# Hybrid decoder layer on one core: half-array products emitted in turn, the overfull test behind the output, and a last norm without GpSimd

## The chip, the core and the metric

The kernel runs on one core of a Trainium2 chip. The metric is the time of one execution in microseconds (us); smaller is better. Everything is float32. The engines are PE (matmuls), DVE (vector), ACT (scalar), POOL (GpSimd) and SP, which here only issues transfers.

## The reference, cut to what matters

One layer over 512 tokens of width 1024: three token mixers in parallel behind one input projection, an output projection and a layer norm, then 32 experts of which each token takes four, and a second layer norm.

```python
p = h @ w_in[l]                                   # 1024 -> all mixers' columns
y_pool = pool_mixer(p_pool, ...)
y_rwkv, v_first = rwkv7_mixer(p_rwkv, ...)        # 6 heads of 64
y_mlstm = mlstm_mixer(p_mlstm, ...)               # 6 heads of 64
mix = jnp.concatenate([y_pool, y_rwkv, y_mlstm], axis=-1) @ w_out[l]
h = layer_norm(DEEPNORM_ALPHA * h + mix, ln1_g[l], ln1_b[l])
ffn = moe_ffn(h, router_w[l], router_b[l], w_gate_up[l], b_gate_up[l], w_down[l], b_down[l])
h = layer_norm(DEEPNORM_ALPHA * h + ffn, ln2_g[l], ln2_b[l])
...
bonus = jnp.sum(rh * kh * rk, -1, keepdims=True) * vh      # in rwkv7_mixer
```

## The kernel before

**Mixer, about 0 to 400 us.** The 512 tokens are four tiles of 128 (`NT`). `x` and the weights are split into a high and a low part, so each product of the input projection is three matmuls (L222 to L224, or L249 to L251 for the mLSTM's values in `ml_vo`). `ml_vo` takes its columns in the rounds 2, 0, 1 of 256; a round holds four PSUM banks, tagged "pi" and "pm", until ACT evacuates them (L256). `self.bank()` alone takes a bank of the tag "ps".

The RWKV part goes over three head pairs `j`. `rwkv_prep(j)` makes the scaled keys and values, the bonus product (L596, evacuated by L597) and then the flips, transposes on PE (L604 and after). `rwkv_scores(j)` makes for each token tile four 128x128 products for each of two heads. A head has 64 features, so each product uses 64 of the array's 128 rows: `hh` 0 the upper half, `hh` 1 the lower (L652). DVE masks the products out of PSUM (L655 to L657), and PE uses the masked tile in L662 and L663. For the last pair, products L637 of both halves come first, in turn. `rwkv_base` is a serial chain of 31 steps on DVE (L693, L695); its result takes a round trip by DMA, is transposed (L699), and `rwkv_inv` begins with L756. `ml_scores` has half-array products of the same kind (L373).

**Experts, about 400 to 1455 us.** 402 MB of weights stream through a ring of SBUF chunks on SP's queue (L1171). Before the ring is free, its chunks are tiles of the mixer, so a load waits until the mixer lets go of its slot. POOL gathers tokens and adds the results to `yd` in DRAM.

**Tail.** `tail_rows` adds `yd` to the four residual tiles `res` by accumulating DMAs (L1507), with the loads of the norm's vectors between them (L1510), all on POOL's queue. `overflow` is an If on the count of the fullest expert (L1408 loads it on each engine, L1409 branches); it is not taken on these inputs. Then `tail`: PE scatters the last expert's results into eight banks (L1524, L1527), DVE adds them to `res` (L1531), ACT sums squares (L1537), and `scales` and `apply` end the norm. Tiles 0 and 1 use ACT (L1559), DVE (L1560) and GpSimd (L1561); tiles 2 and 3 use DVE (L1546, L1557). SP stores each half tile (L1562).

A scheduler decides the order in which each engine gets its instructions; each engine then runs them in that order.

Of the kernel before, what the change touches and what calls it, by code (L numbers as in the profile page):

```python
# [29 lines left out]
AF = mybir.ActivationFunctionType  # L30
# [96 lines left out]
class Trunk:  # L127
# [100 lines left out]
    def ml_vo(self):  # L228
# [9 lines left out]
        for q in (2, 0, 1):  # L238
# [4 lines left out]
            ps = [self.bank("pi" if i < 2 else "pm") for i in range(NT)]  # L243
# [114 lines left out]
    def ml_scores(self, i):  # L358
# [8 lines left out]
        for h in range(6):  # L367
            self.exp_ins = nc.scalar.activation(DW[:, h], DW[:, h], AF.Exp, bias=self.Q[:, i, 0, h:h + 1])
        for g in range(2):
            p = self.bank("pi")  # L370
            r = slice(64 * g, 64 * g + 64)
            for j in range(3):
                nc.tensor.matmul(p[:, j * 128:j * 128 + 128], self.k2[j][r, t], self.q2[j][r, t], start=True, stop=True)  # L373
            d = DW[:, g:6:2]
            nc.vector.scalar_tensor_tensor(d, p[:, :384].rearrange("p (j t) -> p j t", j=3), 1.0 / 32, d, OP.mult, OP.mult)
# [170 lines left out]
    def rwkv_prep(self, j):  # L546
# [12 lines left out]
        nc.tensor.matmul(p, self.w2t[0:64, j * 128:(j + 1) * 128], self.wdad[0:64], start=True, stop=True)  # L559
# [11 lines left out]
        pa = self.bank()  # L571
        nc.tensor.matmul(pa, self.w2t[64:128, j * 128:(j + 1) * 128], self.wdad[64:128], start=True, stop=True)
# [46 lines left out]
        for hh in range(2):  # L619
            rr = slice(64 * hh, 64 * hh + 64)  # L620
            for i in range(NT - 1):
                nc.vector.tensor_copy(self.H[i][rr, j], p[rr, 128 * i:128 * i + 128][:, rr])
        self.pj[j] = (at, bt, kt, cj)

    def rwkv_scores(self, j, first=False):
# [16 lines left out]
        for i in range(NT):  # L642
            ti = slice(i * 128, i * 128 + 128)
            tm = self.sp.tile([128, 2, 2, 128], F32, name="mkv", tag="mkv", bufs=2)
            (mab, mrb), yrk = self.M[i], self.Yrk[i]
            for hh in range(2):
                hd = 2 * j + hh
                rows = slice(64 * hh, 64 * hh + 64)
                p = self.bank()
                for q in range(1 if first else 0, 4):  # L650
                    lh, rh = prods[q]
                    nc.tensor.matmul(p[:, 128 * q:128 * q + 128], lh[rows, ti], rh[rows, ti], start=True, stop=True)  # L652
                pq = p.rearrange("p (q t) -> p q t", q=4)
# [536 lines left out]

    def expert_gather(self, e):
        x = self.xg[e % 2]
        self.nc.gpsimd.indirect_dma_start(out=x[0:CAP], out_offset=None, in_=self.hd,  # L1193
                                          in_offset=bass.IndirectOffsetOnAxis(ap=self.gidx[:, e:e + 1], axis=0),
                                          bounds_check=T - 1, oob_is_err=False)
        return x
# [151 lines left out]
    def experts(self):  # L1348
        self.xg = [self.mw.tile([128, D], F32, name=f"xg{q}") for q in range(2)]
        for x in self.xg:  # L1350
            self.nc.gpsimd.memset(x[0:CAP], 0.0)
# [3 lines left out]
        for e in range(NE):  # L1355
# [36 lines left out]
    def overflow(self):  # L1392
# [15 lines left out]
        most = nc.values_load(self.mxi[0:1, 0:1], min_val=0, max_val=T)  # L1408
        with tc.If(most > CAP):  # L1409
# [102 lines left out]
    def tail(self, out):  # L1512
# [167 lines left out]
```

## Time and profile before

| | |
|---|---|
| median of 3 runs | 1492.03 us (1488.74 to 1493.71) |
| the profiled execution | 1492.41 us |
| its span in the trace | 1490.7 us |
| PE busy | 1345.4 us, 90% |
| DVE, ACT, POOL busy | 466.6, 290.7, 228.2 us |
| data moved | 461.67 MB, 310 GB/s on average |

The span runs from the first to the last event of the trace; the profiled time is 1.7 us longer. Busy shares are averages over the three stages, which have different limits, so they are read stage by stage. Of matmuls the records overlap: two in flight at once count once as busy time, and a record lasts longer than the step from one to the next.

### The profile page before, as it was taken

What the parts mean: (1) busy time and instruction counts of PE and PEld (TensorE: products, weight loads), DVE (VectorE), ACT (ScalarE), POOL (GpSimd) and SP (SyncE); (2) the same over time, 40 slices, a digit from 0 to 9 for tenths busy, and PEclk for the clock granted to TensorE, in tenths of its full rate; (3) what the DMA queues carried; (4) which work ended last, traced back from release to release, by engine and by line L of the source; (5) the groups of instructions that cost most, each with busy time, mean ns of one, the idle gap of its engine ahead of it and who ended that gap; (6) DMA issues with size and microseconds to landing.
All of it is one profiled execution on the core that took longest, in us unless ns stands there. A gap on an engine that the chain in (4) does not pass through costs nothing. (4 is left out here: it accounts for less than half of the span.)

```text
span 1490.7 us, 19988 instructions
## 1 busy us (share of the span) xinstructions
PE 1345.4 (90%) x7852; PEld 639.2 (43%) x7853; DVE 466.6 (31%) x1108; ACT 290.7 (20%) x611; POOL 228.2 (15%) x206
## 2 busy tenths in 40 slices
PE   7899989998899999988799999999879888899993
PEld 5677888876533433232233333333323222333322
DVE  4867497697831212111111111111111110211115
ACT  4444243353211111111001111111100110111103
POOL 1111137142301010001001111011100100010111
PEclk9999888799899999999999999999999999999996
DMA  7222123355689999999999999999999999999964
GB/s 250 70 57 71 36 68 89 118 159 205 256 341 396 393 383 404 402 398 390 395 399 398 394 398 399 402 395 391 392 387 398 395 401 394 404 396 412 401 223 127
DMA packets 95232, 461.67 MB, mean 310 GB/s; under 512 B 18137, under 2 KB 26745, under 8 KB 45962
## 3 DMA queue, kind: packets, MB, share of 16 engines
q1 hardware_dynamic: 79674, 434.57, 74.1%
q0 software_dynamic: 10880, 21.32, 6.6%
q10 hardware_dynamic: 4560, 4.15, 0.9%
q8 instruction: 82, 1.34, 0.4%
q14 instruction: 36, 0.29, 0.1%
HBM read 445.97 MB, written 18.10 MB: 311 GB/s over the span
## 5 line engine op out<-in xcount | busy, mean ns | idle before, releaser
L1268 PE MATMUL gu<-wc,xT 128*64 128x512 f32 x2048 | 486.6, 606 | 67.0 <-DMA wc<-w_gate_up 64.4
L1268 PEld LDWEIGHTS gu<-wc,xT 128*64 128x64 f32 x2048 | 143.0, 138 | 392.9 <-issue 239.5
L1281 DVE TENSOR_SCALAR glu<-gu 128x256 f32<-128x256 f32 (+1 forms) x64 | 35.6, 556 | 843.8 <-PE gu L1273 391.5
L1314 PE MATMUL dn<-wc,aT 128*64 128x512 f32 x1024 | 247.6, 603 | 4.2 <-PEq L1261 2.4
L1282 ACT ACTIVATE glu<-glu 128x256 f32<-128x256 f32 (+1 forms) x64 | 33.6, 525 | 549.6 <-DVE glu L1281 549.4
L1193 POOL DMA_INDIRECT xg<-hd,gidx x31 | 31.3, 1009 | 665.0 <-PE tr L1207 659.7
L1314 PEld LDWEIGHTS dn<-wc,aT 128*64 128x64 f32 x1024 | 65.8, 136 | 117.6 <-issue 101.3
L1319 POOL DMA_INDIRECT yd<-eo,sidx x45 | 70.1, 1557 | 276.1 <-ACT eo L1318 276.1
L1273 PE MATMUL gu<-wc,xT 128*32 128x512 f32 x960 | 111.3, 596 | 0.0
L222 PE MATMUL pi<-xhi,whi 128*128 128x512 f32 x152 | 63.7, 419 | 8.9 <-ACT whi L172 8.9
L1208 ACT ACTIVATE xT<-tr 128x384 f32<-128x384 f32 x62 | 29.9, 490 | 177.2 <-PE tr L1207 177.2
L223 PE MATMUL pi<-xlo,whi 128*128 128x512 f32 x152 | 62.8, 413 | 0.6 <-DVE xlo L173 0.6
L1273 PEld LDWEIGHTS gu<-wc,xT 128*32 128x32 f32 x960 | 27.7, 109 | 79.3 <-issue 79.3
L224 PE MATMUL pi<-xhi,wlo 128*128 128x512 f32 x152 | 61.7, 406 | 0.0
L173 POOL TENSOR_TENSOR wlo<-wraw,whi 128x512 fp32r<-128x512 f32 (+1 forms) x28 | 39.3, 1407 | 134.9 <-ACT whi L172 129.4
L1318 ACT ACTIVATE eo<-dn,gate 128x512 f32<-128x512 f32 (+1 forms) x45 | 28.0, 621 | 162.9 <-PE dn L1314 84.4
L1309 PE MATMUL dn<-wc,aT 128*32 128x256 f32 x960 | 56.1, 381 | 1.0 <-ACT aT L1296 1.0
L172 ACT ACTIVATE whi<-wraw 128x512 fp32r<-128x512 f32 (+1 forms) x54 | 33.9, 631 | 56.4 <-DMA wraw<-w_in 25.3
L1309 PEld LDWEIGHTS dn<-wc,aT 128*32 128x32 f32 x960 | 29.5, 110 | 33.3 <-issue 13.8
L1284 DVE SCALAR_TENSOR_TENSOR glu<-glu 128x256 f32<-128x256 f32 (+1 forms) x64 | 35.6, 556 | 8.4 <-ACT glu L1282 7.1
L1295 PEld LDWEIGHTS tr<-ident,glu 128*128 128x128 f32 x192 | 25.7, 208 | 28.0 <-DVE sel L1214 19.5
L222 PEld LDWEIGHTS pi<-xhi,whi 128*128 128x128 f32 x152 | 29.5, 194 | 18.2 <-ACT whi L172 8.6
(489 smaller groups left out, 1585.8 us busy)
## 6 DMA issues: line engine op xcount, KB each, us to landing
wc<-w_gate_up SPq DMA_DIRECT2D x256, 1024.0 KB
wc<-w_down SPq DMA_DIRECT2D x128, 1024.0 KB
wraw<-w_in SPq DMA_DIRECT2D x46, 256.0 KB
wraw<-w_out SPq DMA_DIRECT2D x16, 256.0 KB
xraw<-xT SPq DMA_DIRECT2D x4, 512.0 KB
res<-x SPq DMA_DIRECT2D x4, 512.0 KB
hd<-res ACTq DMA_DIRECT2D x4, 512.0 KB
res<-yd POOLq DMA_DIRECT2D x4, 512.0 KB
```

Of the source, the lines that this page charges most:

```text
L172: self.hi_ins = nc.scalar.activation(hi, src, AF.Copy)
L173: return (eng or nc.vector).tensor_tensor(lo, src, hi, OP.subtract)
L222: nc.tensor.matmul(p, hi, xh, start=(k == 0), stop=False)
L223: nc.tensor.matmul(p, hi, xl, start=False, stop=False)
L224: nc.tensor.matmul(p, lo, xh, start=False, stop=(k == NK - 1))
L1268: mm(p[q][64 * h:64 * h + 64], xT[:, k, 0:64], w[:, 1024 * q + 512 * h:1024 * q + 512 * h + 512], start=False, stop=(k == NK - 1))
L1273: self.nc.tensor.matmul(p[2][32 * c:32 * c + 32], xT[:, k, 64:96], w4[:, c], start=False, stop=(k == NK - 1), skip_group_check=True)
L1281: nc.vector.tensor_scalar(out[:, c], g, 7.0, None, OP.min)
L1284: nc.vector.scalar_tensor_tensor(out[:, c], ln[:, c], 1.0, out[:, c], OP.add, OP.mult)
L1309: mm(p2[32 * c:32 * c + 32], aT[:, 4 + k % 2, 32 * (k // 2):32 * (k // 2) + 32], wd[k][:, 256 * c:256 * c + 256], start=(k == 0), stop=(k ...
L1314: mm(p0[64 * h:64 * h + 64], aT[:, k % 4, 64 * (k // 4):64 * (k // 4) + 64], wd[k][:, 512 * h:512 * h + 512], start=(k == 0), stop=(k == N ...
L1319: return nc.gpsimd.indirect_dma_start(out=self.yd.rearrange("t (c f) -> (t c) f", f=w), out_offset=bass.IndirectOffsetOnAxis(ap=self.sidx[ ...
```

## The change

- `rwkv_scores` and `ml_scores` take both banks first and emit the products of the two halves in turn.
- `ml_vo`'s round 0, the second of the three, takes four "ps" banks in place of "pi" and "pm".
- `rwkv_prep` emits the bonus product and its evacuation behind the flips. Its two products with `w2t` are written side by side.
- The two zeroed gather tiles of the experts go, and the first gathers have no bounds check.
- The overfull test is emitted behind the tail. If it is taken, it redoes the norm and stores again.
- The norm's vectors are loaded on SP's queue in `tail_setup`, not on POOL's between the accumulating DMAs.
- The last norm: `res` of tiles 2 and 3 is added by PE, as a product with the identity, and ACT reads the sum out of PSUM. All four tiles are centred, scaled and shifted by DVE into new tiles. Tiles 0 and 1 share one reciprocal square root, 2 and 3 another. GpSimd does nothing there.

```diff
@@ ml_vo
-            ps = [self.bank("pi" if i < 2 else "pm") for i in range(NT)]
+            ps = [self.bank("ps" if q == 0 else "pi" if i < 2 else "pm") for i in range(NT)]
@@ rwkv_prep
         nc.vector.scalar_tensor_tensor(r, r, self.col("rk", j), k, OP.mult, OP.mult)
-        p = self.bank()
-        nc.tensor.matmul(p[32 * j:32 * j + 2], c["bd2"], r, start=True, stop=True)
-        nc.scalar.activation(self.bonT[32 * j:32 * j + 2], p[32 * j:32 * j + 2], AF.Copy)
...
                 nc.vector.tensor_copy(self.H[i][rr, j], p[rr, 128 * i:128 * i + 128][:, rr])
+        p = self.bank()
+        nc.tensor.matmul(p[32 * j:32 * j + 2], c["bd2"], r, start=True, stop=True)
+        nc.scalar.activation(self.bonT[32 * j:32 * j + 2], p[32 * j:32 * j + 2], AF.Copy)
@@ rwkv_scores
+            ps = [self.bank() for _ in range(2)]
+            for q in range(1 if first else 0, 4):
+                lh, rh = prods[q]
+                for hh in range(2):
+                    rows = slice(64 * hh, 64 * hh + 64)
+                    nc.tensor.matmul(ps[hh][:, 128 * q:128 * q + 128], lh[rows, ti], rh[rows, ti], start=True, stop=True)
             for hh in range(2):
                 hd = 2 * j + hh
-                rows = slice(64 * hh, 64 * hh + 64)
-                p = self.bank()
-                for q in range(1 if first else 0, 4):
-                    lh, rh = prods[q]
-                    nc.tensor.matmul(p[:, 128 * q:128 * q + 128], lh[rows, ti], rh[rows, ti], start=True, stop=True)
@@ overflow(out), in the If, for each tile
                 nc.sync.dma_start(self.ow[i][:, 0:1024], self.yo[i * 128:i * 128 + 128])
-                nc.vector.tensor_tensor(self.res[i], self.res[i], self.ow[i][:, 0:1024], OP.add)
+                nc.vector.tensor_tensor(r, r, self.ow[i][:, 0:1024], OP.add)
+                self.ln_apply(r, self.ln_stats(self.mw, r), self.g2, self.b2)
+                d = nc.sync.dma_start(out[i * 128:i * 128 + 128], r)
@@ tail_setup
+        for t, src in ((self.g2, self.a["ln2_g"]), (self.b2, self.a["ln2_b"])):
+            nc.sync.dma_start(t, bass.AP(tensor=src.tensor, offset=src.offset, ap=[[0, 128], [1, D]]))
@@ tail
+                if i > 1:
+                    mm(p, self.ident, self.res[i][:, hs[q]], start=True, stop=False)
...
+                if i > 1:
+                    nc.scalar.activation(r[:, f], ps[i][q], AF.Identity, accum_out=col(q))
+                else:
+                    nc.vector.scalar_tensor_tensor(r[:, f], ps[i][q], 1.0, r[:, f], OP.mult, OP.add, accum_out=col(q))
...
+                nc.vector.scalar_tensor_tensor(xs[i][:, f], self.res[i][:, f], st[:, i, 2:3], self.g2[:, f], OP.add, OP.mult)
...
-                    nc.scalar.activation(r[:, f], r[:, f], AF.Identity, bias=col(8), scale=col(6))
-                    nc.vector.tensor_tensor(r[:, f], r[:, f], self.g2[:, f], OP.mult)
-                    nc.gpsimd.tensor_tensor(r[:, f], r[:, f], self.b2[:, f], OP.add)
...
+                nc.vector.scalar_tensor_tensor(xs[i][:, f], xs[i][:, f], st[:, i, 6:7], self.b2[:, f], OP.mult, OP.add)
+                self.stores[i].append(nc.sync.dma_start(out[i * 128:i * 128 + 128, f], xs[i][:, f]))
@@ trunk
-                t.overflow()
                 t.tail(out)
+                t.overflow(out)
```

Three places on PE. A row is a line, an operation, its output and inputs, and the shape; "x4" stands for four of them. In `rwkv_prep` of the second head pair, the order before, with the bonus product L596 ahead of the flips (L604, L613):

```order
L223 MATMUL pi_901<-xlo0_88,whi_847 128x512
L224 MATMUL pi_901<-xhi0_86,wlo_848 128x512
L596 MATMUL ps_707<-M2_232,cst_62 2x512
L604 MATMUL ps_710<-ident_60,M3_233 128x128 x4
L604 MATMUL ps_716<-ident_60,prep_559 128x128 x4
L604 MATMUL ps_722<-ident_60,prep_558 128x128 x4
L613 MATMUL ps_728<-ident_60,prep_558 128x128 x4
```

The same place after, where the flips are L602 and L611, and the bonus product L622:

```order
L602 MATMUL ps_713<-ident_60,prep_559 128x128 x4
L224 MATMUL pi_858<-xhi1_87,wlo_669 128x512
L222 MATMUL pi_901<-xhi0_86,whi_847 128x512
L223 MATMUL pi_901<-xlo0_88,whi_847 128x512
L224 MATMUL pi_901<-xhi0_86,wlo_848 128x512
L222 MATMUL pi_901<-xhi0_86,whi_847 128x512
L602 MATMUL ps_719<-ident_60,prep_558 128x128 x4
L611 MATMUL ps_725<-ident_60,prep_558 128x128 x4
L223 MATMUL pi_901<-xlo0_88,whi_847 128x512
L616 MATMUL ps_734<-Vt_223,prep_558 128x128 x3
L622 MATMUL ps_744<-M2_232,cst_62 2x512
```

The bonus product moved behind all flips, with projection products (L222 to L224) between them.

In the `rwkv_scores` that follow, the order before for one token tile; ps_748 and ps_756 are the banks of the two halves:

```order
L652 MATMUL ps_748<-prep_237,prep_238 128x128
L652 MATMUL ps_748<-Vt_223,prep_238 128x128
L652 MATMUL ps_748<-prep_237 128x128
L652 MATMUL ps_748<-Vt_223,prep_237 128x128
L652 MATMUL ps_756<-prep_237,prep_238 128x128
L652 MATMUL ps_756<-Vt_223,prep_238 128x128
L652 MATMUL ps_756<-prep_237 128x128
L652 MATMUL ps_756<-Vt_223,prep_237 128x128
L223 MATMUL pi_901<-xlo0_88,whi_847 128x512
```

And after, with ps_748 and ps_749 as the two banks:

```order
L652 MATMUL ps_748<-prep_237,prep_238 128x128
L652 MATMUL ps_749<-prep_237,prep_238 128x128
L652 MATMUL ps_748<-Vt_223,prep_238 128x128
L652 MATMUL ps_749<-Vt_223,prep_238 128x128
L652 MATMUL ps_748<-prep_237 128x128
L652 MATMUL ps_749<-prep_237 128x128
L652 MATMUL ps_748<-Vt_223,prep_237 128x128
L652 MATMUL ps_749<-Vt_223,prep_237 128x128
L224 MATMUL pi_901<-xhi0_86,wlo_848 128x512
L222 MATMUL pi_901<-xhi0_86,whi_847 128x512
L223 MATMUL pi_901<-xlo0_88,whi_847 128x512
```

The products alternate between the halves, and more projection products follow them.

At the end of the program, before: the last expert's products (L1314, L1309), one scatter group (L1524, L1527), and the test:

```order
L1314 MATMUL dn0_9913<-wc_9780,aT_9839 64x512 x4
L1309 MATMUL dn2_3901<-wc_9780,aT_9839 32x256 x8
L1524 MATMUL dn2_10532<-wc_9830 128x512
L1524 MATMUL dn2_10532<-wc_9832,wc_9830 128x512
L1527 MATMUL dn2_10532<-wc_9831 128x256 x4
L1408 TENSOR_LOAD mxi_3550
L1409 COMPARE_AND_BRANCH
```

The other seven scatter groups stood behind the If. After, the last two groups of eight, with the identity products L1527 (the scatter products are L1529 and L1532 now), and the test behind them:

```order
L1527 MATMUL dn0_10021<-res1_2754,ident_60 128x512
L1529 MATMUL dn0_10021<-wc_9838 128x512
L1529 MATMUL dn0_10021<-wc_9840,wc_9838 128x512
L1532 MATMUL dn0_10021<-wc_9839,wc_9838 128x256 x2
L1532 MATMUL dn0_10021<-wc_9839 128x256 x2
L1527 MATMUL dn2_10022<-res1_2754,ident_60 128x512
L1529 MATMUL dn2_10022<-wc_9838 128x512
L1529 MATMUL dn2_10022<-wc_9840,wc_9838 128x512
L1532 MATMUL dn2_10022<-wc_9839 128x256 x4
L1383 TENSOR_LOAD mxi_3548
L1410 COMPARE_AND_BRANCH
```

The test moved behind all scatter groups; on DVE and ACT it likewise stands behind the norm.

## Rows read from the trace of the kernel before

**Rows 1.** The page: its first line.

```profile
span 1490.7 us, 19988 instructions
...
```

**Rows 2.** Stretches: length, busy us by engine, granted clock, DMA share, GB/s.

```profile
...
100.00:200.00 100.00, 97.20 (x579) 81.79 (x579) 63.32 (x153) 37.82 (x90) 18.79 (x18) 0.91 0.21 53
...
430.00:440.00 10.00, 9.22 (x52) 3.49 (x46) 4.03 (x11) 1.71 (x4) 0.00 (x0) 1.00 1.01 386
600.00:1000.00 400.00, 370.83 (x2183) 125.81 (x2180) 51.20 (x120) 43.64 (x88) 39.49 (x30) 1.00 1.02 397
...
```

**Rows 3.** SyncE in time: the first weight loads; start, us, line.

```profile
...
339.66 48.48 SPq L1171 DMA_DIRECT2D wc<-w_gate_up  x13
...
```

**Rows 4.** What PE waited for, whole run: us in total, times, longest.

```profile
...
PE ps L596 <- DVE M L594: 7.4, 3, 3.7
...
PE gu L1524 <- PEq L1409: 6.1, 1, 6.1
...
```

**Rows 5.** PE in time: one token tile of L652, then products L637.

```profile
...
101.02 0.48 PE L652 MATMUL ps<-prep 64*128 64x128 f32 x2
...
102.35 0.38 PE L652 MATMUL ps<-Vt,prep 64*128 64x128 f32 x2
...
164.16 0.71 PE L637 MATMUL ps<-prep 64*128 64x128 f32 x8
```

**Rows 6.** DVE in time: the masking of one token tile.

```profile
...
109.41 0.29 DVE L655 TENSOR_TENSOR M<-ps,cst 128x128 f32<-128x128 f32 x1 [1.95 <-PE ps L652]
...
110.55 0.41 DVE L657 TENSOR_TENSOR mkv<-ps,cst 128x256 f32<-128x256 f32 x1
...
```

**Rows 7.** Two ten-us stretches of the mixer, columns as in rows 2.

```profile
...
170.00:180.00 10.00, 10.00 (x50) 8.75 (x49) 4.31 (x11) 0.89 (x4) 0.55 (x1) 0.59 0.37 66
200.00:210.00 10.00, 10.00 (x86) 9.90 (x85) 9.52 (x18) 5.06 (x8) 2.74 (x2) 1.00 0.30 80
...
```

**Rows 8.** PE, then POOL in time: round 1 of `ml_vo` and its last weights.

```profile
...
216.81 0.58 PE L249 MATMUL pi<-whi,xhi 128*128 128x256 f32 x1 [6.70 <-ACT V L256]
...
219.62 1.30 POOL L173 TENSOR_TENSOR wlo<-wraw,whi 128x512 fp32r<-128x512 f32 x1 [1.77 <-ACT whi L172]
```

**Rows 9.** The serial chain and its user: ns, first and last start.

```profile
...
L693 DVE TENSOR_TENSOR bb<-ba x31: 179/356/1470, 188.4 to 225.6; 96x31 f32<-96x31 f32 x2, 96x60 f32<-96x60 f32 x2, 96x87 f32<-96x87 f32 x2, 96x112 f32<-96x112 f32 x2
...
L756 PE MATMUL ps<-bb,M x96: 191/192/257, 242.8 to 248.4; 32*32 32x32 f32 x96
...
```

**Rows 10.** Two stretches of the tail, columns as in rows 2.

```profile
...
1462.00:1464.00 2.00, 1.36 (x4) 1.20 (x5) 0.00 (x0) 0.00 (x0) 0.00 (x0) 0.50 1.10 233
1464.00:1470.00 6.00, 6.00 (x27) 5.34 (x26) 2.88 (x8) 1.52 (x4) 0.00 (x0) 0.60 0.03 6
...
```

**Rows 11.** The test by engine: ns, first and last start.

```profile
...
L1409 SPq EVENT_SEMAPHORE  x9: 17/17/17, 1431.0 to 1445.6; - x9
...
L1409 SPq COMPARE_BRANCH  x1: 45/45/45, 1425.7 to 1425.7; - x1
...
L1409 PEldq COMPARE_BRANCH  x1: 6362/6362/6362, 1456.0 to 1456.0; - x1
...
```

**Rows 12.** PE in time: two scatter groups of the tail.

```profile
...
1470.16 0.63 PE L1524 MATMUL tr<-wc 128*128 128x512 f32 x2
...
1471.10 0.63 PE L1524 MATMUL dn<-wc 128*128 128x512 f32 x2
...
```

**Rows 13.** Line L596: a float32 product of 512 columns; ns.

```profile
...
L596 PE MATMUL ps<-M,cst x6: 589/590/706, 54.9 to 145.9; 128*2 128x512 f32 x6
...
```

**Rows 14.** The tail in time, all engines.

```profile
...
1467.41 0.72 ACT L1537 ACTIVATE wc<-res,tst 128x512 f32<-128x512 f32 x1 [11.17 <-DVE tst L1535]
...
1475.57 3.42 POOL L1561 TENSOR_TENSOR res<-res,wc 128x512 f32<-128x512 f32 x2 [22.30 <-DVE tst L1551]
...
1476.10 1.76 DVE L1546 SCALAR_TENSOR_TENSOR wc<-res,tst,wc 128x512 f32<-128x512 f32 x1
...
1485.91 1.41 DVE L1557 SCALAR_TENSOR_TENSOR res<-wc,tst 128x512 f32<-128x512 f32 x2
```

More of the change, by code (lines that the diff above doesn't have):

```diff
@@ L368, in ml_scores @@
             self.exp_ins = nc.scalar.activation(DW[:, h], DW[:, h], AF.Exp, bias=self.Q[:, i, 0, h:h + 1])
+        ps = [self.bank("pi") for _ in range(2)]
+        for j in range(3):
+            for g in range(2):
+                r = slice(64 * g, 64 * g + 64)
+                nc.tensor.matmul(ps[g][:, j * 128:j * 128 + 128], self.k2[j][r, t], self.q2[j][r, t], start=True, stop=True)
         for g in range(2):
[L370 to L373, printed above, removed]
             d = DW[:, g:6:2]
-            nc.vector.scalar_tensor_tensor(d, p[:, :384].rearrange("p (j t) -> p j t", j=3), 1.0 / 32, d, OP.mult, OP.mult)
+            nc.vector.scalar_tensor_tensor(d, ps[g][:, :384].rearrange("p (j t) -> p j t", j=3), 1.0 / 32, d, OP.mult, OP.mult)
         if i < NT - 1:
@@ L558, in rwkv_prep @@
         p = self.bank()
-        nc.tensor.matmul(p, self.w2t[0:64, j * 128:(j + 1) * 128], self.wdad[0:64], start=True, stop=True)
+        pa = self.bank()
+        for o, rows in ((p, slice(0, 64)), (pa, slice(64, 128))):
+            nc.tensor.matmul(o, self.w2t[rows, j * 128:(j + 1) * 128], self.wdad[rows], start=True, stop=True)
         nc.vector.memset(sg[:, :, 0:1], 0.0)
@@ L1192, in expert_gather @@
         x = self.xg[e % 2]
+        some = {} if e < 3 else dict(bounds_check=T - 1, oob_is_err=False)
         self.nc.gpsimd.indirect_dma_start(out=x[0:CAP], out_offset=None, in_=self.hd,
[L1194 to L1195 removed]
+                                          in_offset=bass.IndirectOffsetOnAxis(ap=self.gidx[:, e:e + 1], axis=0), **some)
         return x
@@ L1381, in experts @@
             if e == NE - 1:
+                self.most = self.nc.values_load(self.mxi[0:1, 0:1], min_val=0, max_val=T)
                 self.tail_setup()
@@ L1389, in experts, with overflow @@
         self.dn(*pend)
-    def overflow(self):
+    def overflow(self, out):
         nc, tc = self.nc, self.tc
@@ L1407, in overflow @@
         self.nw = 0
-        most = nc.values_load(self.mxi[0:1, 0:1], min_val=0, max_val=T)
-        with tc.If(most > CAP):
+        with tc.If(self.most > CAP):
             nc.vector.memset(self.oone, 1.0)
@@ L1522, in tail @@
                 p = ps[i][q]
+                if i > 1:
+                    mm(p, self.ident, self.res[i][:, hs[q]], start=True, stop=False)
                 for z in range(2):
-                    mm(p, self.P[q][:, t], self.slast[z], start=z == 0, stop=False)
+                    mm(p, self.P[q][:, t], self.slast[z], start=i < 2 and z == 0, stop=False)
                 for x in range(2):
@@ L1527, in tail @@
                         mm(p[:, 256 * x:256 * x + 256], self.P[2 + 2 * q + x][:, t], self.slast[2 + z], start=False, stop=x == z == 1)
+        s = [self.chunk()[0] for _ in range(2)]
+        xs = [s[i // 2][:, 1024 * (i % 2):1024 * (i % 2) + 1024] for i in range(NT)]
+        self.stores = [[] for _ in range(NT)]
         def add(i):
```

57 lines of the change are left out of this document (16 added, 41 removed).

## The prediction

> **What bounds the kernel now.** I read the page's first line for the span [rows 1], then the stretches, since each stage has a limit of its own [rows 2]. From 430 us the transfers take 1.01 of the sixteen engines' time, and from 600 to 1000 us 1.02, at 397 GB/s; PE is busy 370.83 of those 400 us. The experts are bound by the stream of weights, and an edit to PE there would give nothing. What counts is when the stream starts and what follows it. The mixer sets the start: from 100 to 200 us PE is busy 97.20 of 100 us while transfers take 0.21 of theirs, and thirteen of the first weight loads are issued over 48.48 us from 339.66 us, as slots of the mixer come free [rows 3]. The bytes are fixed, so a microsecond less in the mixer starts the stream a microsecond earlier and should reach the end whole. Behind the stream comes the tail, where DVE is busy 17.15 of the last 21 us and PE 2.20 [rows 2].
>
> PE's waits name two places that the change touches: 7.4 us at the bonus product L596, and 6.1 us at L1524 for the branch of the test [rows 4]. A third, in `ml_vo`, comes below.
>
> **Scores.** A tile's L652 has sixteen records (two per float32 product). The first starts at 101.02 us, the last at 102.46 (two from 102.35 take 0.38, and a record lasts 0.27): with the step to the next, 1.55 us, mostly one after the other [rows 5]. The products L637 alternate halves already: eight records take 0.71 us from the first start to the last end [rows 5]. So their starts span 0.44: four pairs, some 0.11 apart. Sixteen in turn should take 0.9 to 1.0 us, about 0.65 less. Eight tiles of the first two pairs: 5.2 us. Bound below: DVE masks both halves in 1.55 us, from 109.41 to 110.96 [rows 6]. Now it can start only when nearly all products are done, and PE must have other work for that long. The new order puts projection products behind the scores (seven behind the first tile), so most of it is covered; if 0.45 of each 0.65 is lost, 1.6 us remain. I take 5.2. The last pair has twelve records a tile, and from 170 to 180 us the granted clock is 0.59, near the lower of its two levels, 1.2 GHz [rows 7]. At full clock twelve records save 0.5 us a tile, at that level some 0.8: one and three tiles, 2.9 us; without overlap at half clock, 0.5. L373 has twelve records in each of four tiles; that lies behind the chain below, and I count nothing (0 to 2).
>
> The Trainium skill, in "TensorEngine Tiling (Array Packing)", section "PSUM Bottleneck", warns that faster tiled products can leave the evacuation of PSUM as the limit. By it, the lower bound would be the likelier value, and the forecast below 3.6 us later, 1466. The trace bears out that DVE's 1.55 us per tile is longer than PE's new 1.0 [rows 6], and leaves open whether other work covers it.
>
> **Bonus.** L596 waits 7.4 us for DVE, three times, the longest 3.7 [rows 4], and the flips stand behind it. Moved back, it finds its input done; the flips may then wait for theirs, also from DVE. If the longest of the waits stays there, 3.7 are left of the gain; I leave them 1.4: 6.0 us (3.7 to 7.4).
>
> **Round 0 of `ml_vo`.** Round 1 waited 6.7 us, until 216.81, for ACT to evacuate the banks of the round before [rows 8]. With "ps" banks it needs no evacuation of the round just ahead. What is late next is its own weights: the last of four pieces is split on POOL from 219.62 us for 1.30, and PE reached the round at 210.1 [rows 8]. A round is 96 products (8 blocks, 4 banks, 3 lines), at 86 in 10 us [rows 7] 11.2 us, so three quarters last until 218.5 and PE waits 2.4 for the last if POOL's split does not move. It stands behind DVE work that comes earlier with the rest. 5.5 us, between 4.3 and 6.7.
>
> Sum of the mixer: 5.2 + 2.9 + 6.0 + 5.5 = 19.6 us. The cap is the serial chain, steps from 188.4 to 226 us [rows 9]. It starts after the scores and bonus products, 14.1 us earlier by these terms. `rwkv_inv` starts at 242.8 us, 17 us behind the chain's last step [rows 9]; between them lies the round trip, and I take some 6 us of the 17 as PE's projections alone, so the chain allows about 20. The sum stays just under it. Bounds from the terms: 10.1 and 20.
>
> **Tail.** Before, two 512-KB loads stood between the four accumulating ones. Transfers end about 1464 us, at 233 GB/s [rows 10]. Without those 1.05 MB they end 4.5 us earlier, about 1459.5. PE resumed only at 1462.64, as its branch took 6.36 us from 1456.0 [rows 11]. Now all groups follow the first, which was done when the branch began. A group takes 0.94 us (1470.16 to 1471.10) [rows 12]. Four plain ones end at 1456.2 + 3 x 0.94 = 1459.0; each of the others has an identity product more, two records of 0.59 at L596's price, 1.1 us [rows 13]. 1459.0 + 4 x 2.04 = 1467.2. ACT then reads the sum (0.72 and a read-out of 0.2, by its square of that size [rows 14]), squares two halves (1.8), the root and its five steps take 1.3, and DVE applies four halves of 0.71: 1474.0. DVE's own work is as long: eight centrings and eight applications of 0.71, four additions of as much, some 2.5 of small steps: 16.7 us from 1457. Before, the last application ended at 1487.32; GpSimd ran 3.42 us from 1475.57, and a DVE instruction beside it took 1.76, where two of that shape took 1.41 later [rows 14]. From 1474.0 to 1487.32 are 13.3 us. I take off 2 for two chains of one length that meet, and 1 for the test at the end: 10 us (4 to 13).
>
> The test at the end has a price on each engine. PE's 6.36 us now start about 1467 and lie beside DVE's last work. On SP the branch took 45 ns, but its next event came 5.3 us later, at 1431.0 [rows 11]; part may be a wait. Beside the landing of the last store, 3.4 us from 1487.32 to the span's end, 0 to 3 us remain.
>
> **At nothing.** The zeroed tiles and the bounds check are POOL work under the experts, which wait for weights; uncovered, they would give up to 5.2 us, as two tiles of 1024 columns are four POOL operations of 1.30 [rows 8]. The two products with `w2t` were adjacent before. The vectors' loads on SP go behind the last weights, with some 20 us to spare.
>
> Sum: 1492.4 - 19.6 - 10 = 1462.8 for a profiled execution of 1492.41 us; the median of the runs is 0.4 lower. Forecast **1462.5 us**.
>
> **Rivals.**
> - *Scores and chain give less.* DVE's masking paces the tiles, flips wait in the bonus product's place, round 1 waits for weights: 1.6 + 0.5 + 3.7 + 4.3 = 10.1 us, then 1472. For: DVE's 1.55 against PE's 1.0. Against: the projection products between.
> - *The branch at the end is paid in the open.* SP or DVE fetches the far target with nothing beside it, 6.4 us as on PE, 3.4 of them under the store: the tail gives 7 in place of 10, and the time is 1465.5. The Trainium skill, in "Runtime: NRT & Kernel Launch", section "Instruction fetch mechanics", says that a taken branch to code outside the window makes the engine wait for a transfer. PE's 6.36 us agree, the 45 ns of SP's do not by themselves.
> - *The mixer's gain is not passed on.* The loads wait for slots by another clock than PE's, or the stream's start is set by routing: 1492.4 - 10 = 1482. Against: transfers are at 0.21 in the mixer.
> - *Slower.* The granted clock falls: it was 0.59 from 170 to 180 us, soon after the products L637 that alternate halves at 164.16 [rows 5, 7]. Work that falls from the upper level (2.4 GHz) to the lower takes twice as long, so each us of it costs one. From 30 us on the gain is gone. If half of the 100 us from 100 us on fell, the kernel would take 1512. Against: in that stretch, with some of these products in it, the clock was 0.91 [rows 2].
> - *The pairs do not overlap* at 128 columns and the rest holds: 8.1 us less, 1470.5.
>
> **How the numbers follow.** The forecast with the bounds of its terms (1454 to 1468), 0.55, and in it 0.10 for the branch in the open. Less from scores and chain, or no overlap (1468 to 1476), 0.24. Not passed on (1476 to 1487), 0.10. The clock (over 1487), 0.06, half of it within 0.3%. Under 1454, if the clock rises where PE no longer waits, 0.05. The range for 8 in 10 is 1453 to 1480. A measurement here can't tell changes within 0.3%, 4.5 us, from none. Faster 0.94, same 0.03, slower 0.03.
>
> **What would show it.** L652's sixteen records within 1.0 us; no wait at L622 and under 3 us at L249; `rwkv_inv` near 223 us; the stream of weights at 1.0 share some 20 us earlier; PE without a gap behind 1455 (earlier by the mixer's gain) and its last group 12 us later; DVE instructions of 0.71 to 0.75 to the end. The forecast is wrong if the chain does not start 14 us earlier, if the granted clock falls in the scores, or if more than 5 us lie between DVE's last application and the span's end.

## The result, and the profile after

The changed kernel takes 1473.63 us (median of 4 runs, 1472.02 to 1473.74) against 1491.47 us before: a ratio of 0.9879, 95% interval 0.986 to 0.9897, so 17.8 us less. The time lies in the range that was given, but 11 us above the forecast: of the 29.6 us that I added up, 17.8 came. The profiled execution takes 1473.74 us, its span 1472.0.

The stretches, with the columns of [rows 2]:

```profile
...
100.00:200.00 100.00, 97.41 (x673) 82.11 (x672) 72.07 (x161) 41.61 (x92) 23.45 (x22) 1.00 0.24 62
170.00:180.00 10.00, 10.00 (x84) 9.39 (x84) 6.58 (x21) 2.68 (x9) 2.73 (x6) 1.00 0.15 27
210.00:220.00 10.00, 5.13 (x15) 4.10 (x16) 7.46 (x17) 2.99 (x12) 4.25 (x7) 0.66 0.50 96
230.00:240.00 10.00, 4.30 (x91) 3.89 (x91) 9.01 (x16) 2.65 (x6) 9.92 (x11) 0.60 0.26 71
420.00:430.00 10.00, 9.13 (x50) 3.48 (x44) 3.57 (x11) 1.70 (x4) 0.00 (x0) 1.00 1.02 393
600.00:1000.00 400.00, 375.17 (x2250) 128.75 (x2248) 51.10 (x120) 44.41 (x90) 40.05 (x30) 0.99 1.02 397
...
```

The transfers reach a share of 1.02 from 420 us, ten microseconds earlier than before, and keep the same 397 GB/s behind it [rows 2]. From 170 to 180 us, where the clock was 0.59 [rows 7], it is 1.00. PE, however, is busy only 5.13 of the ten microseconds from 210 us and 4.30 from 230 us.

What PE waited for in the whole run (total, times, longest):

```profile
...
PE pi L222 <- ACT so L259: 7.0, 1, 7.0
PE pi L373 <- DVE ks L291: 5.7, 1, 5.7
...
PE tr L1527 <- DMA res<-yd: 2.6, 1, 2.6
...
PE ps L602 <- DVE prep L592: 2.2, 2, 1.1
PE ps L602 <- DVE M L504: 2.2, 2, 1.6
PE ps L602 <- DVE prep L589: 1.9, 3, 0.6
...
```

The waits at the bonus product, at L249 and at the branch are gone [rows 4, 8]. In their place stand 7.0 us at the next projection L222, which needs the banks that ACT's L259 empties, 5.7 us at L373, which needs `ks` from DVE, 2.6 us in the tail for the landing of `res`, and 6.3 us in all at the flips L602.

The chain and its user, by line (ns, first and last start):

```profile
...
L695 DVE TENSOR_TENSOR bb<-ba x31: 178/370/1440, 175.2 to 212.8; 96x31 f32<-96x31 f32 x2, 96x60 f32<-96x60 f32 x2, 96x87 f32<-96x87 f32 x2, 96x112 f32<-96x112 f32 x2
...
```

```profile
...
L758 PE MATMUL ps<-bb,M x96: 191/224/257, 228.4 to 238.6; 32*32 32x32 f32 x96
...
```

The chain starts 13.2 us earlier than in [rows 9], and the first product behind it 14.4 us earlier. The last of the 96 products starts only 9.8 us earlier: this step lasts 10.2 us where it lasted 5.6. An early first product lengthens the step by itself, since half of the 96 start at once and the others stand behind L373, which waits for `ks`:

```profile
...
228.43 1.40 PE L758 MATMUL ps<-bb,M 32*32 32x32 f32 x48
...
235.94 0.79 PE L373 MATMUL pi<-qs,ks 64*128 64x128 f32 x2 [5.70 <-DVE ks L291]
...
```

From the chain's start to the last of the 96, both parts together, are 63.4 us in place of 60.0.

The scores of the first tile, and the tail on PE, in time:

```profile
...
97.33 0.49 PE L652 MATMUL ps<-prep 64*128 64x128 f32 x4
97.66 0.39 PE L652 MATMUL ps<-Vt,prep 64*128 64x128 f32 x4
97.88 0.39 PE L652 MATMUL ps<-prep 64*128 64x128 f32 x4
98.10 0.39 PE L652 MATMUL ps<-Vt,prep 64*128 64x128 f32 x4
...
```

```profile
...
1449.43 1.13 PE L1527 MATMUL tr<-res,ident 128*128 128x512 f32 x2 [2.59 <-DMA res<-yd]
...
1451.88 1.91 PE L1527 MATMUL tr<-res,ident 128*128 128x512 f32 x2
...
1454.75 1.02 PE L1527 MATMUL dn<-res,ident 128*128 128x512 f32 x2
...
1456.55 1.02 PE L1527 MATMUL dn<-res,ident 128*128 128x512 f32 x2
...
```

Sixteen records start between 97.33 and 98.22 us; with the step to the next that is 1.0 us, as forecast from L637, against 1.55 in [rows 5]. In the tail the first identity product waits 2.59 us for `res` and takes 1.13; the second takes 1.91, at a clock that fell just behind the wait, and the last two, with the clock up again, 1.02:

```profile
...
1448.00:1450.00 2.00, 0.57 (x3) 0.33 (x3) 2.00 (x6) 2.00 (x7) 0.00 (x0) 1.00 1.07 213
1450.00:1452.00 2.00, 2.00 (x9) 1.62 (x8) 1.38 (x4) 0.76 (x3) 0.00 (x0) 0.66 0.24 45
1452.00:1454.00 2.00, 2.00 (x4) 0.88 (x3) 0.00 (x0) 0.69 (x2) 0.00 (x0) 0.50 0.00 0
1454.00:1456.00 2.00, 2.00 (x10) 1.41 (x9) 0.34 (x2) 0.96 (x4) 0.00 (x0) 0.99 0.03 8
...
```

DVE's last operations, and the test at the end by engine:

```profile
...
1455.66 0.21 DVE L1545 TENSOR_SCALAR tst<-tst 128x1 f32<-128x1 f32 x1 [4.25 <-ACT res L1542]
...
1463.45 2.74 DVE L1561 SCALAR_TENSOR_TENSOR wc<-wc,tst 128x512 f32<-128x512 f32 x4
```

```profile
...
L1410 SPq EVENT_SEMAPHORE  x9: 17/17/17, 1469.7 to 1470.3; - x9
...
L1410 PEldq COMPARE_BRANCH  x1: 3321/3321/3321, 1454.9 to 1454.9; - x1
...
L1410 SPq COMPARE_BRANCH  x1: 45/45/45, 1466.6 to 1466.6; - x1
...
```

DVE stood idle for 4.25 us, ended by ACT's reading of tile 2, and finished at 1466.19 us. SyncE branches at 1466.6, its next events come at 1469.7, and the span ends at 1472.0: 5.8 us behind DVE, where it was 3.4. That is more than the 5 us which I had named as a sign that the forecast is wrong. A second such sign came as well: the chain starts 13.2 us earlier, not 14. The third did not: the clock stayed up in the scores.

### The profile page after: what moved, and what is told of

Same layout as the page of the kernel before. It is cut to its first block, busy times and chain, and to the rows that moved or that the text cites. A ratio compares the mean times of both kernels' runs of the same rounds, so it can differ in the third digit from the quotient of the medians.

```text
span 1472.0 us, 19986 instructions
## 1 busy us (share of the span) xinstructions
PE 1332.8 (91%) x7860; PEld 625.3 (42%) x7861; DVE 459.8 (31%) x1094; ACT 289.1 (20%) x613; POOL 217.9 (15%) x198
## 3 DMA queue, kind: packets, MB, share of 16 engines
q10 hardware_dynamic: 4560, 4.15, 1.0%
## 5 line engine op out<-in xcount | busy, mean ns | idle before, releaser
L222 PE MATMUL pi<-xhi,whi 128*128 128x512 f32 x152 | 64.4, 423 | 15.9 <-ACT whi L172 8.9
L224 PE MATMUL pi<-xhi,wlo 128*128 128x512 f32 x152 | 62.0, 408 | 0.0
L222 PEld LDWEIGHTS pi<-xhi,whi 128*128 128x128 f32 x152 | 29.3, 193 | 26.2 <-ACT whi L172 8.8
```

What stands on the lines that cost most here:

```text
L222: nc.tensor.matmul(p, hi, xh, start=(k == 0), stop=False)
L224: nc.tensor.matmul(p, lo, xh, start=False, stop=(k == NK - 1))
```

## The experiments

An execution of one kernel varies by some microseconds: the changed kernel, run again, took 1477.69 us (1476.18 to 1480.53) beside a kernel before of 1490.28, a gain of 12.6 us and not 17.8. So I read each experiment from stretches of its profile, of which there is one for each kernel. This table is worked out from starts in the traces: the first record of L652; from it to the chain's first step; from there to the first of the 96 products of `rwkv_inv`; from the first to the last of them; from there to the first expert product; from there to the first accumulating issue; and from that to the span's end (the tail). All in us.

| kernel | first L652 | to chain | to inv | inv step | to experts | experts | tail | span |
|---|---|---|---|---|---|---|---|---|
| before | 101.0 | 87.4 | 54.4 | 5.6 | 150.0 | 1049.8 | 42.5 | 1490.7 |
| changed | 97.3 | 77.9 | 53.2 | 10.2 | 149.3 | 1050.1 | 34.0 | 1472.0 |
| a0 changed, again | 99.6 | 77.8 | 53.5 | 10.2 | 153.1 | 1050.7 | 34.0 | 1478.8 |
| e1 banks undone | 98.2 | 77.9 | 51.5 | 9.7 | 152.4 | 1050.4 | 34.1 | 1474.3 |
| e2 scores undone | 97.9 | 88.2 | 53.7 | 6.0 | 151.0 | 1050.5 | 34.2 | 1481.4 |
| e3 bonus undone | 100.6 | 77.1 | 53.6 | 10.2 | 153.3 | 1050.5 | 34.3 | 1479.7 |
| e4 mixer only | 97.2 | 77.7 | 53.8 | 8.3 | 152.0 | 1049.8 | 42.0 | 1480.7 |
| e6 last pair undone | 98.3 | 77.7 | 53.6 | 7.2 | 152.6 | 1050.4 | 34.3 | 1474.1 |
| e7 two pairs undone | 97.6 | 81.2 | 53.7 | 7.5 | 149.0 | 1050.2 | 34.2 | 1473.5 |
| e8 test ahead | 98.5 | 77.7 | 53.7 | 10.2 | 153.2 | 1049.7 | 36.1 | 1479.1 |
| m1 scaling held | 99.1 | 77.9 | 53.8 | 5.2 | 148.1 | 1051.2 | 34.1 | 1469.4 |
| t1 root early | 98.7 | 77.9 | 54.0 | 9.3 | 151.1 | 1051.0 | 34.3 | 1476.3 |
| t2 identity undone | 98.6 | 77.9 | 53.7 | 6.1 | 150.6 | 1050.9 | 31.4 | 1469.2 |
| b1 m1 and t2 | 96.7 | 78.0 | 53.8 | 5.4 | 150.6 | 1050.1 | 31.3 | 1465.8 |

The experts' column is 1049.7 to 1051.2 in all fourteen: what the mixer gains passes through the stream whole. The twelve kernels that do the same work up to the first L652 reach it at 96.7 to 99.6 us, so 2 or 3 us in that column are not clear of noise.

**a0.** 

> The changed kernel once more, unaltered, beside the kernels of this call. Both theories: 1473.6 within 3 us; the tail, from the first accumulating issue to the span's end, 34.0 us.

1477.69 us, ratio 0.9911 (0.9879 to 0.9943): 4.1 us above the first result, so the expected 3 us did not hold; the tail is the same. a0, e6, e7 and e8 ran on one chip, the other experiments on another, so what is chip and what execution is not told apart. This execution is 6.8 us longer than the first: 2.3 up to the first L652, 3.8 between `rwkv_inv` and the experts. Its clock was 0.91 from 60 to 80 us and 0.91 from 320 to 360, where the first had 1.00 in both:

```profile
...
60.00:80.00 20.00, 17.71 (x64) 12.16 (x64) 10.50 (x21) 10.08 (x20) 5.03 (x4) 0.91 0.20 53
320.00:360.00 40.00, 34.17 (x156) 26.01 (x154) 27.19 (x82) 12.74 (x34) 6.68 (x7) 0.91 0.53 182
...
```

**e1, round 0 of `ml_vo` back on "pi" and "pm".**

```diff
-            ps = [self.bank("ps" if q == 0 else "pi" if i < 2 else "pm") for i in range(NT)]
+            ps = [self.bank("pi" if i < 2 else "pm") for i in range(NT)]
```

> The changed kernel, with round 0 of ml_vo back on the banks pi and pm. Theory A (the serial chain on DVE and what DVE does behind it set the mixer's end; PE's wait only moved from L249 to the next projection, L222, 7.0 us): the time stays at 1473.6 within 2 us, the wait of some 6.7 us is back at L249, rwkv_inv starts within 1 us of 228.4. Theory B (PE's waits add up, as in my sum): 1479, 5.5 us more, and rwkv_inv near 234.

1476.32 us, ratio 0.9909 (0.9874 to 0.9945). A wait of 5.0 us is back at L249, and that at L222 is gone:

```profile
...
PE pi L373 <- DVE ks L291: 5.2, 1, 5.2
PE pi L249 <- ACT V L256: 5.0, 1, 5.0
```

From the first L652 to the first product of `rwkv_inv` are 129.4 us against 131.1: no later, even a little earlier. The time lies 2.7 us above what theory A expects and 2.7 below theory B, and decides nothing; the stages do. Theory A stands: this edit gives nothing here.

**e2, the scores half by half again.** Only `rwkv_scores` is as before the change.

```diff
-            ps = [self.bank() for _ in range(2)]
-            for q in range(1 if first else 0, 4):
-                lh, rh = prods[q]
-                for hh in range(2):
-                    rows = slice(64 * hh, 64 * hh + 64)
-                    nc.tensor.matmul(ps[hh][:, 128 * q:128 * q + 128], lh[rows, ti], rh[rows, ti], start=True, stop=True)
             for hh in range(2):
...
+                p = self.bank()
+                for q in range(1 if first else 0, 4):
+                    lh, rh = prods[q]
+                    nc.tensor.matmul(p[:, 128 * q:128 * q + 128], lh[rows, ti], rh[rows, ti], start=True, stop=True)
```

> The changed kernel, with the products of rwkv_scores again half by half (ml_scores stays in turn). Theory A: the chain starts later by what the pairs are worth, up to 8.1 us by my terms (5.2 and 2.9), near 183 in place of 175.2, and the whole shows in the time: about 1481. Theory B (DVE's masking paced the tiles, so turn-taking gave 2 us): 1475.5, and the chain near 177.

1480.71 us, ratio 0.9931 (0.9911 to 0.9951). From the first L652 to the chain are 10.2 us more than in the changed kernel, where my terms had 8.1, and the step of `rwkv_inv` is 6.0. The clock fell behind 169 us:

```profile
...
170.00:180.00 10.00, 10.00 (x43) 8.86 (x42) 2.80 (x8) 0.61 (x3) 0.00 (x0) 0.50 0.22 32
180.00:190.00 10.00, 10.00 (x59) 9.78 (x60) 4.86 (x14) 2.44 (x8) 2.57 (x5) 0.69 0.12 25
...
```

This is one of ten executions, and one of the three longest: 1483.23 us, with a mean clock of 0.967. Three took 1475.05 to 1475.88 at 0.974 to 0.976, so the fall may not come each time.

**e6 and e7, one part of the scores half by half.** Both keep the two banks taken up front; the condition is `first` (the last pair) in e6 and `not first` in e7.

```diff
-            for q in range(1 if first else 0, 4):
+            qs = range(1 if first else 0, 4)
+            for q, hh in [(q, hh) for hh in range(2) for q in qs] if first else [(q, hh) for q in qs for hh in range(2)]:
                 lh, rh = prods[q]
-                for hh in range(2):
...
```

> The changed kernel, with the products of the last head pair again half by half, those of the first two pairs in turn. With all three undone the chain started at 186.0 and the granted clock was at its lower level for 17 us behind 170 us. Theory A (the clock falls behind the last pair's products, when they go half by half): the 17 us at the lower level are back, the chain starts near 183 (8 us of clock), the time is near 1479. Theory C (only the products' own time counts, the clock's fall is by chance of the stretch): the chain starts at 177 to 178 and the clock stays up.

1476.27 us, ratio 0.9901 (0.9862 to 0.9939). The clock stayed up and the chain started at 176.1, 77.7 us behind the first L652: the last pair's products alone are worth nothing there. Theory A fell.

> The changed kernel, with the products of the first two head pairs again half by half, those of the last in turn. Theory A: the clock stays at its upper level behind 170 us, and the chain starts later by the first two pairs' own time alone, 3 to 5 us: 178 to 180, and the time is 1477. Theory C: the same without the clock's part in the other run; if instead the fall of the clock comes back here, it hangs on the first two pairs and the chain starts at 184 or later.

1480.62 us, ratio 0.9933 (0.9911 to 0.9955). This profile is of the fastest of six executions, 1475.21 us; the others took 1480.40 to 1481.42. The clock stayed up here too, from 170 to 180 us 1.00 in both, e6 and then e7:

```profile
...
170.00:180.00 10.00, 10.00 (x79) 9.06 (x78) 6.40 (x20) 2.80 (x9) 2.40 (x5) 1.00 0.19 38
...
```

```profile
...
170.00:180.00 10.00, 10.00 (x84) 9.40 (x83) 4.86 (x15) 2.46 (x9) 1.23 (x4) 1.00 0.29 46
...
```

The chain comes 3.3 us later: the first two pairs' own time, where I had 5.2. So of the 10.2 us some 7 came with the clock (in e2 ten microseconds at 0.50 and ten at 0.69 cost 5.0 and 3.1 us of full-clock work). It fell there in the profiles of the two kernels where all of L652 went half by half (before and e2), in none of the other twelve. That the order of the products brings it down is argued from these fourteen profiles, not shown; why neither part alone does stays open. Beside a0, on the same chip, the times agree with the stages: e6 lies 1.4 us below it, e7 2.9 above.

**e3, the bonus product ahead of the flips again.** Its three lines go back from the end of `rwkv_prep` to their place before the change:

```diff
         nc.vector.scalar_tensor_tensor(r, r, self.col("rk", j), k, OP.mult, OP.mult)
+        p = self.bank()
+        nc.tensor.matmul(p[32 * j:32 * j + 2], c["bd2"], r, start=True, stop=True)
+        nc.scalar.activation(self.bonT[32 * j:32 * j + 2], p[32 * j:32 * j + 2], AF.Copy)
...
```

> The changed kernel, with the bonus product ahead of the flips again. Theory A: the waits at the bonus product return (7.4 us before; flips now wait 3.5), the chain starts 4 to 6 us later, the time is 1478 to 1480. Theory B (the flips wait for DVE anyway, so the order is worth nothing): 1474, with the chain at 175 to 176.

1477.99 us, ratio 0.992 (0.9892 to 0.9948). PE waits 7.1 us at the bonus product again. But the first L652 comes at 100.6, between 1.0 and 3.9 us later than in the twelve kernels with the new order, and behind it nothing is lost (77.1). So the edit is worth some 2 to 3 us, between the two theories, and hardly more than the noise of that column. The first of the waits, in the kernel before and then in e3:

```profile
...
54.87 1.13 PE L596 MATMUL ps<-M,cst 128*2 128x512 f32 x2 [3.66 <-DVE M L594]
...
```

```profile
...
54.42 1.75 PE L597 MATMUL ps<-M,cst 128*2 128x512 f32 x2 [3.44 <-DVE M L595]
...
```

Behind it the clock fell in both, to 0.91 on average from 40 to 60 us; in the twelve others it is 1.00 there. So part of the 2 to 3 us is clock: 0.91 over 20 us is 1.8 us less of full-clock work.

**e4, the mixer's edits alone.** The kernel before, with `ml_vo`, `ml_scores`, `rwkv_prep` and `rwkv_scores` of the change.

> The kernel before with the edits of the mixer alone; experts and tail as before. If mixer and tail are independent, the first accumulating issue comes at 1438 as in the changed kernel, and the time is 1491.5 - 10.2 = 1481.3. If the tail's edits also moved the mixer or the experts (SyncE's queue, slots), it lies elsewhere; if nothing of the mixer's gain reached the end, 1491.

1483.41 us, ratio 0.9951 (0.9929 to 0.9972). The first accumulating issue comes at 1438.7, and the tail is 42.0 us: mixer and tail are independent.

**e8, the test ahead of the tail again.** The body of the If only adds, as before the change.

```diff
-                t.tail(out)
                 t.overflow(out)
+                t.tail(out)
```

> The changed kernel, with the overfull test ahead of the tail again (its body as before: it only adds). Theory A (the wait for the last accumulating transfers, 11.4 us behind the first issue, bounds the changed tail, and PE's branch of 3.3 to 6.4 us runs beside it): the tail takes 34 to 36 us in place of 34.0, since 2.4 us come back at the end and PE starts some 4 us late. Theory B (the branch was the tail's bound, as in my working): the tail takes 39 to 40 us, and the time is 1479.

1479.8 us, ratio 0.9926 (0.9903 to 0.9949), 2.1 us above a0. The tail is 36.1. PE's branch took 6.87 us and ended at 1454.2, 11.3 us behind the first accumulating issue, about as late as the wait for `res` ends in the changed kernel (11.4); at the end only 3.3 us follow DVE's last operation. The move is worth some 2 us net, near theory A.

**m1, POOL's scaling by the bonus held back.** `xt_dve` is DVE's last copy into XT.

```diff
-                    nc.vector.tensor_copy(s12[b, :, b], src)
+                    self.xt_dve = nc.vector.tensor_copy(s12[b, :, b], src)
...
+            self.after(d, self.xt_dve, mybir.DependencyClass.Sync)
```

> The changed kernel, with POOL's scaling of V by the bonus (L840, L844) held until DVE has written the last block of XT, behind the chain. In the changed kernel the two ran side by side from 230.58 us, and DVE's copies there took 0.90 and 2.12 us where the kernel before had 0.56 and 1.14; PE then waited 5.7 us at L373 for ks. Theory A (DVE's copies were held up by POOL's two-input operations): the copies take 0.6 and 1.1 us again, L373 waits 1.5 to 2 us less, and from the first L652 to the last product of the first step of rwkv_inv are 139.5 us in place of 141.3. Theory B (the copies were late for their inputs, or PE's order alone makes the wait): nothing changes, 141.3.

1473.71 us, ratio 0.9893 (0.9869 to 0.9918). DVE in time, the changed kernel and then m1:

```profile
...
230.72 0.90 DVE L724 COPY XT<-bb 32x384 f32<-32x384 f32 x1
231.54 0.97 DVE L729 COPY X<-bb 32x384 f32<-32x384 f32 x1
232.53 2.12 DVE L724 COPY XT<-bb 32x384 f32<-32x384 f32 x2
234.69 1.20 DVE L291 SCALAR_TENSOR_TENSOR ks<-cv 128x512 f32<-128x512 f32 x1
...
```

```profile
...
230.66 0.35 DVE L724 COPY XT<-bb 32x384 f32<-32x384 f32 x1
230.94 0.65 DVE L729 COPY X<-bb 32x384 f32<-32x384 f32 x1
231.60 1.46 DVE L724 COPY XT<-bb 32x384 f32<-32x384 f32 x2
233.09 0.69 DVE L291 SCALAR_TENSOR_TENSOR ks<-cv 128x512 f32<-128x512 f32 x1
...
```

And POOL beside it in the changed kernel:

```profile
...
230.58 1.73 POOL L840 TENSOR_TENSOR Vt<-Vt,bon 128x384 f32<-128x384 f32 x2
232.27 2.17 POOL L844 TENSOR_TENSOR Vt<-Vt,lora 128x384 f32<-128x384 f32 x2
...
```

The same copies take 0.90, 0.97 and 2.12 us beside L840 and L844, and 0.35, 0.65 and 1.46 without them. In the changed kernel they end as a POOL instruction has ended: the second at 232.51 us, 0.20 behind the end of L840, the last at 234.65, 0.21 behind the end of L844. L373 waits 1.3 us, and from the first L652 to the last product of the step are 137.0 us in place of 141.3. Theory A stands.

Not all of this is the edit's. From the first copy above to the end of `ks` are 5.17 us in the changed kernel and 3.12 in m1: 2.05 us, as theory A expected. But these copies also began earlier, 53.7 us behind the chain's start in place of 55.5, and in t2, which leaves this part of the kernel as it is, they began at 53.8: there L373 waits 1.9 us, and the step is 6.1. So 2.05 us are the scaling's. This loss follows the moment at which POOL starts it: 2.3 us behind the first of these copies in e2 and t2, 1.9 in e6 and e7, 1.3 in e1 and e4, 0.4 in t1, and 0.1 ahead of it in the changed kernel, a0, e3 and e8; to the end of `ks` are 3.63, 4.17, 4.67, 4.84 and 5.17 us. Why the copies begin later in some kernels stays open. The medians, 1473.71 us here and 1473.63 and 1477.69 for the changed kernel, show no gain by themselves.

**t1, the root of tiles 0 and 1 ahead of ACT's reading of tile 2.** `scales` and `apply` of the first pair come before `add` of tiles 2 and 3, and ACT's reading stands behind the root.

```diff
-        i = nc.scalar.activation(y, v, AF.Sqrt, bias=self.eps[eps])
+        i = self.root = nc.scalar.activation(y, v, AF.Sqrt, bias=self.eps[eps])
...
-                    nc.scalar.activation(r[:, f], ps[i][q], AF.Identity, accum_out=col(q))
+                    d = nc.scalar.activation(r[:, f], ps[i][q], AF.Identity, accum_out=col(q))
+                    self.after(d, self.root)
...
-        for f, i in ((add, 0), (add, 1), (centre, 0), (add, 2), (centre, 1), (add, 3), (scales, 0), (apply, 0), (apply, 1),
+        for f, i in ((add, 0), (add, 1), (centre, 0), (centre, 1), (scales, 0), (apply, 0), (apply, 1), (add, 2), (add, 3),
...
```

> The changed kernel, with the root of tiles 0 and 1 ahead of ACT's reading of tiles 2 and 3. In the changed kernel DVE stood idle for 4.25 us in the tail, as the root was queued on ACT behind two readings that wait for PE. Theory A (PE's last products, behind the landing of res at 11.4 us and partly at the lower clock, bound the tail): the idle time is used, but the tail shrinks by 0.5 to 1.5 us alone, 32.5 to 33.5 in place of 34.0. Theory B (DVE's own 17 us are the bound): the 4.25 us come back, 30 us.

1475.33 us, ratio 0.9894 (0.9871 to 0.9916). The tail is 34.3: the idle time moved, and not even the 0.5 to 1.5 us of theory A came of it. DVE's work is not the bound; PE's last group ends 20.4 us behind the first accumulating issue, where it ended 20.5.

**t2, no identity product.**

```diff
-                if i > 1:
-                    mm(p, self.ident, self.res[i][:, hs[q]], start=True, stop=False)
...
-                if i > 1:
-                    nc.scalar.activation(r[:, f], ps[i][q], AF.Identity, accum_out=col(q))
-                else:
+                if True:
                     nc.vector.scalar_tensor_tensor(r[:, f], ps[i][q], 1.0, r[:, f], OP.mult, OP.add, accum_out=col(q))
```

> The changed kernel, with res of all four tiles added by DVE and no identity product. Theory A (PE's four identity products behind the landing bound the tail): PE is done before the landing, DVE adds tiles 2 and 3 as they land, and the tail takes 32 to 33 us in place of 34.0. Theory B (the identity products relieve DVE, which is the bound): four more additions of 0.77 on DVE, 36 to 37 us.

1473.42 us, ratio 0.989 (0.9866 to 0.9913). The tail is 31.4, 2.6 less and a little more than theory A expected. DVE adds tile 2 from 1449.58, as it lands, and waits no more:

```profile
...
1449.58 0.69 DVE L1540 SCALAR_TENSOR_TENSOR res<-tr,res 128x512 f32<-128x512 f32 x1
...
1452.25 0.69 DVE L1540 SCALAR_TENSOR_TENSOR res<-dn,res 128x512 f32<-128x512 f32 x1
...
```

**b1, m1 and t2 together.**

> The changed kernel with both edits that shortened a stage: POOL's scaling by the bonus held until DVE has written XT, and res of all four tiles added by DVE. If the two are independent: 137 us from the first L652 to the last product of the first step of rwkv_inv (141.3 in the changed kernel), 31.4 us from the first accumulating issue to the end (34.0), and a time 5 us below the changed kernel's, 1469 to 1473. Rival (the mixer's 4 us are swallowed by the clock or the stream, as not all of them showed before): 2.6 us below, 1471 to 1475.

1467.49 us (1467.36 to 1469.61) beside 1488.32 before, ratio 0.9853 (0.9826 to 0.988). Both stages are as short as in m1 and t2, 137.2 us from the first L652 to the last product of the step and 31.3 for the tail, and the time lies below the expected 1469 to 1473: the fastest of these kernels.

## Why the prediction was right, and where its terms were off

**The number.** Direction and range are right, the sum is not: 10.2 us in place of 19.6 from the mixer, 8.5 in place of 10 from the tail. The time lies 1.6 us from the rival in which scores and chain give less (1472), but that is luck: of its terms, 1.6 + 0.5 + 3.7 + 4.3, the scores gave more, the bonus less and round 0 nothing, and a loss behind the chain, which it does not have, came on top.

**What bounds.** Right: the stream starts ten microseconds earlier and takes as long as before, so the mixer's gain reaches the end whole. The rival that denied this is refuted by the experts' column and by e4.

**Scores.** Own time 3.3 us for the first two pairs in place of 5.2, and nothing for the last in place of 2.9. But the clock that fell behind them before stayed up, some 7 us that I had not counted; the term of 8.1 came out as 10.2, near it by luck. The rival in which alternation lowers the clock is refuted: the profiles have it the other way round.

**Bonus.** 2 to 3 us in place of 6.0: the flips wait 6.3 us for DVE (I left them 1.4), where the bonus product had waited 7.4. The 1.1 us between them and up to 1.8 us of clock behind the first of the old waits make up what was gained.

**Round 0 of `ml_vo`.** 0 in place of 5.5, the step that failed outright. I took the wait at L249 as PE's own loss, and let "6 of the 17 us" behind the chain fall to PE's projections. But from the chain's start to `rwkv_inv` are 53.2 to 54.4 us in all kernels but e1 (51.5). The wait moved to L222, whose banks ACT's L259 empties, and L259 stands on ACT's queue behind the issue of the round trip, L699, which waits for the chain's last step:

```profile
...
213.30 1.02 ACTq L699 DMA_DIRECT2D xd<-ba  x2
...
214.55 0.27 ACT L259 ACTIVATE so<-pi 128x128 f32<-128x128 f32 x1
...
```

So PE's projections still follow the chain, and the cap of 20 was 13 to 14.

**What I did not see.** From the chain's start to the last of the 96 products the changed kernel takes 3.4 us more than the kernel before. DVE ended `ks` 60.7 us behind the chain's start in place of 57.7: its copies began 1.2 us later, and from the fifth on they and `ks` took 5.17 us in place of 3.3, since POOL's scaling now ran beside them. In the kernel before it began only behind `ks`, at 246.57 us:

```profile
...
242.76 0.56 DVE L722 COPY XT<-bb 32x384 f32<-32x384 f32 x1
...
245.39 0.69 DVE L291 SCALAR_TENSOR_TENSOR ks<-cv 128x512 f32<-128x512 f32 x1
...
```

The Trainium skill, "SBUF — State Buffer", section "SBUF: two separate sides", says that VectorE and GpSimd share a pair of SBUF ports as an exclusive lock: of a VectorE instruction in a two-port mode and a GpSimd instruction, whichever starts first gets the pair for its whole instruction, and the other blocks. The trace agrees: beside L840 and L844 two copies end 0.20 and 0.21 us behind the end of a POOL instruction, and 0.35 us became 0.90. That the copies run in such a mode is in no view here.

**Mixer.** 3.7 to the first L652 and 9.5 to the chain, 3.4 given back from there to the last of the 96 products, 0.7 gained and 0.3 lost behind it: 10.2 us in place of 19.6.

**Tail.** 8.5 in place of 10. DVE's last operation came 11.0 us earlier behind the first accumulating issue, where my sum without the test at the end has 11.3. Its parts were off both ways: the transfers ended some 12.4 us behind that issue in place of some 16 [rows 10], 3.6 earlier where I had 4.5; PE ended at 1458.5, 1.5 us later than my sum (1467.2 less the mixer's 10.2), as it waited for `res` and the clock fell just behind that wait; from there to DVE's last operation are 7.7 us, where I had 6.8 and 2 for chains that meet. The branch in the open, a rival, came true in size: 2.4 us more behind DVE's last operation, where I had 1 and the rival 3, yet the move gains some 2 net. That DVE's work was an equally long chain was wrong (t1); the identity products on PE cost more than they saved DVE (t2).

**Left untried or open.** The gathers, the zeroed tiles and the vectors' queue were not taken apart, nor was the new norm: what the queue, the shared root and the norm without GpSimd each give in the tail is argued from the sum, not shown. `ml_scores` and the two products with `w2t` were not undone by themselves.

## What to carry to other kernels

A wait that is removed on one engine is a gain only if the engine that ended it is not on the path: ask what the released engine needs next, and from whom. Measure a stage by events in its trace that do not depend on the rest, when the total varies more than the edit is worth. The step of `rwkv_inv` is a trap of this kind: its first product came early, which made the step longer and lost nothing. Pulling a chain forward changes what runs beside it; look at the durations of the operations on DVE where GpSimd is busy.

## What was not expected of the hardware

- The granted clock stayed at 1.00 from 170 to 180 us where products on the two halves of the array went in turn, in part or in whole (a0, e6, e7), and fell to 0.59 and 0.50 where all went half by half (before, e2), in one profile of each. PE had hardly a longer wait just ahead of it in the one than in the other: 0.57 us before, 0.49 after.
- The same kernel gave spans of 1472.0 and 1478.8 us. The first expert product came 6.1 us later in the second; what the granted clock fell short of 1.00 up to 440 us adds up to 27.3 us in the first and 32.4 in the second, 5.1 of these 6.1.
- PE's branch to the end took 6.36 us before, 6.33 in e4 and 6.87 in e8, where it stands ahead of the tail, and 3.32 to 4.15 in the eleven kernels where it stands behind it; the other engines' took 45 to 76 ns each.
- A DVE copy of 32x384 took 0.35 us alone and 0.90 beside POOL's scaling of 128x384 (m1 and the changed kernel).
